# Two-level products from the first output block on, and a finished row scaled later

## The chip, the cores and the metric

The kernel runs on one core of a Trainium2 chip. The metric is the device time of one execution in microseconds; the median of three runs is 907.44 us (906.86 to 908.13). In the text PE is TensorE, DVE is VectorE, ACT is ScalarE, POOL is GpSimd and SP is SyncE, whose queue issues most of the transfers.

## The reference

With the sizes of this case (one sequence of 4096 frames, width 1024, one layer) only the pooling mixer is left. What is computed, in its essence:

```python
normed = rms_norm(x, norm_w)
u, gate = split(normed @ pool_in_w, 2)                # 1024 -> 2 x 1024
pooled = [trailing_mean(u_g, w) for w in (2, 4, 8, 16)] - u    # four groups of 256 channels
mixed = einsum('bsgc,gcd->bsgd', pooled, pool_group_w) + pool_group_b
h = x + (mixed * pool_scale * silu(gate)) @ pool_out_w         # 1024 -> 1024
out = rms_norm(h, final_norm_w)
```

All in float32.

## The kernel before

**Precision and products.** A float32 operand is split into a high and a low part, both in the type that TensorE multiplies at one column per step (`split`, line 203: the high part is a copy by ScalarE, the low part a subtraction by VectorE). A product is then three matmuls: high by high, high by low, low by high (`mm3`, line 802). Above that the kernel multiplies 2 x 2 blocks with seven products instead of eight (the Winograd form of Strassen's scheme). The seven are called P1 to P7; each needs sums of operand blocks, which VectorE forms, and the results are added up in PSUM and by VectorE and ScalarE.

**Stages.** The list `steps` (line 1439) has one entry for each product: stage a (input product, first half of the output columns) for four input blocks of 1024 frames, stage b (the second half) for the same four, then stage o (the output product) for eight output blocks of 512 frames. The order within an input block is P1, P2, P7, P6, P5, P4, P3 (`ORDER_IN`), within an output block P1, P7, P6, P2, P5, P4, P3 (`ORDER_OUT`). The main loop (line 1882) goes through the steps; at step n it issues the loads of a step some places ahead, the splits of the next one or two steps, and then the matmuls and evictions of step n. Pooling (`pool`, line 1060) runs between input and output: it takes the evicted input product and stores `yd`, which the output blocks load again. In the last input block (stage b, block 3) each step, once its product is done, also loads and splits the output weights of the same name into the same place (`load_w`, line 384).

**A second level.** Some products are themselves done with seven smaller products, so that 24 matmuls of 512 columns become 42 of 256. In the output stage P2 is done so from block 1 on (called the inner P2), and P7 from block 2 on (`OWN = 2`). The inner P2 takes three plain quarters and four sums of its operand (`split_inner`, line 890: four sums of 256 elements and the split of the plain operand; the split of the sums follows one step later, as `rest`). Its weights are three plain quarters of the split weight P2 and four sums, formed by `load_inner` (two loads from `wod`), `sum_inner` (four sums of 512 elements), `split_weight` (for each sum a copy by ScalarE and a subtraction by VectorE into a kept buffer, or, for P5, into a quarter of the weight's own place), and `end_weights` (the two raw buffers are given back). The products of the inner P2 go partly into the banks of the step (`sets["x"]`) and partly into two spare banks; `add_inner` (line 989) adds the spare banks to the rows. P5 and P6 of the inner level are done within the step P5 of the outer one, into a spare bank that `add_inner` has to read first.

**Buffers.** Eleven work buffers (`st`) and eight larger ones (`vt`) are handed out oldest first by `Slots`. `take` and `give` are calls of the program that issues the kernel, so a buffer that is taken again makes the new writer wait until the last reader of the old contents is done. `st.keep()` withdraws a buffer for good, as a home of inner weights; the list `gathered` holds them, three for P2 and, from block 1 on, three more for P7.

**Order.** Each engine works through a queue in order. The queue is written by a list scheduler (called the planner here) that follows a clock of its own: whenever an engine is free by that clock, it places the earliest instruction of the program whose inputs are there. `tc.issue_after` puts an instruction behind another of the same engine. From two steps ahead of output block 2 on, `InOrder.on` keeps the instructions of VectorE, ScalarE, POOL and SP in the order of the program; in the last block it is switched off in the step P2 (line 1607).

**The last block.** `steady` (line 1509) writes out the output blocks from 2 on and the last two steps of block 1. Rows of a finished block are scaled in the next one: `norm_row` (line 1261) multiplies a row group by its factor and the final weight on VectorE and has POOL store it. In the last block one of these, for the block before it, stands in the step P2 ahead of the product and its eviction. After the last product the rows of the last block are scaled by ScalarE and VectorE in halves and stored (`late_scalar`, `late_vector`).

Of the kernel before, what the change touches and what calls it, by code (L numbers as in the profile page):

```python
# [20 lines left out]
NB = S // TB  # L21
# [7 lines left out]
OWN = 2  # L29
# [57 lines left out]
def kernel(  # L87
# [57 lines left out]
    st = Slots(sts)  # L145
# [738 lines left out]
    def end_weights(i):  # L884
        for u in raws.pop(i)["held"]:
            give(u)
# [304 lines left out]

    def split_o(b, i):
        s = oxs[b]
        if i == P2 and b >= OWN - 1:
            return split_inner(s["12"])
        t = next_op("p (s a b) -> p s a b", s=2, a=4)
        if i == P7:
            s["3"] = take("p (a b) -> p a b", a=4)
            sub(s["3"], s["11"], s["21"])
        elif i == P6:  # L1200
            add(s["21"], s["21"], s["22"])
            sub(s["11"], s["21"], s["11"])
        elif i == P3:
            sub(s["12"], s["12"], s["11"])
            give(s.pop("11"))
        key = {P1: "11", P7: "3", P6: "11", P2: "12", P5: "21", P4: "22", P3: "12"}[i]
        split(t, s[key])
        if i not in (P1, P6, P2):
            give(s.pop(key))
        return t  # L1210
# [298 lines left out]
    def steady(n):  # L1509
# [58 lines left out]
        elif i == P6:  # L1568
            v = temp(0, "p (n k c) -> p n k c", n=4, k=2)
            sums_op = next_op("p (s n k c) -> p s n k c", s=2, n=4, k=2)  # L1570
            high(sums_op, v)
            low(sums_op, v)
            own_add()
            u = s.pop("21")
            give(u)
            if final:
                add_out(b, P6, sets, 0)
            norm_row(b - 1, 0, 0)
            if not final:
                norm_row(b - 1, 0, 1)  # L1580
            for m, p in enumerate((P7, P6, P5, P3)):
                ready[P2][p] = [sums_op[:, k, m] for k in range(2)]
            ready[P5] = next_op("p (s a b) -> p s a b", **whole)
            with tc.issue_after(latest[0]):
                out_part(P6, ready.pop(P6), sets["y"][1], 1, range(4))
            if final:
                partial["junk"] = temp(1, "p (a b) -> p a b", a=2)
                add_out(b, P6, sets, 1)
                split(ready[P5], u)
                for j in range(2):  # L1590
                    add_out(b, P7, sets, j)
            else:
                split(ready[P5], u)
                load_h(b, 1)
                evict_o(b, P7, sets)
                evict_o(b, P6, sets)
        elif i == P2:
            if not final:
                load_h(b, 0)
                ahead["11"] = load_y(c, 0, 0)  # L1600
                ahead["21"] = load_y(c, 1, 0)
            ready[P4] = next_op("p (s a b) -> p s a b", **whole)
            split(ready[P4], s["22"])
            give(s.pop("22"))
            if final:
                norm_row(b - 1, 0, 1)
            InOrder.on = not final
            product_out(P2, ready.pop(P2), sets, False)
            evict_o(b, P2, sets)
        elif i == P5:  # L1610
            sub(s["12"], s["12"], s["11"])
            give(s.pop("11"))
            ready[P3] = next_op("p (s a b) -> p s a b", **whole)
            split(ready[P3], s["12"])
            give(s.pop("12"))
            product_out(P5, ready.pop(P5), sets, False)
            evict_o(b, P5, sets)
        elif i == P4:
            if not final:
                ahead["12"] = load_y(c, 0, 1)  # L1620
                ahead["22"] = load_y(c, 1, 1)
                ready[P1] = next_op("p (s a b) -> p s a b", **whole)
                split(ready[P1], ahead["11"])
                u = temp(0, "p (a b) -> p a b", a=4)
                sub(u, ahead["11"], ahead["21"])
                ready["own"] = op_halves()
                high(ready["own"][1], u)
            product_out(P4, ready.pop(P4), sets, False)
            if final:
                evict_o(b, P4, sets)  # L1630
            else:
                add_out(b, P4, sets, 0)
        else:
            if not final:
                u = temp(0, "p (a b) -> p a b", a=4)
                v = temp(1, "p (n k c) -> p n k c", n=4, k=2)
                b11, b12, b21, b22 = row_quarters(u)
                square_rows(b, 1, sets, 0)
                sub(v[:, 0], b12, b11)
                sub(v[:, 1], b22, v[:, 0])  # L1640
                sub(v[:, 2], b22, b12)
                sub(v[:, 3], b21, v[:, 1])
                add_out(b, P4, sets, 1)
                sums_op = next_op("p (s n k c) -> p s n k c", s=2, n=4, k=2)
                high(sums_op, v)
                square_rows(b, 1, sets, 1)
                root(b, 1)
                plain_op, both = ready.pop("own")
                low(both, u)
                low(sums_op, v)  # L1650
                ready[P7] = {
                    p: [plain_op[:, k, g, j] for k in range(2)]
                    for p, (g, j) in {P1: (0, 0), P2: (1, 0), P3: (1, 1)}.items()
                }
                for m, p in enumerate((P5, P6, P7, P4)):
                    ready[P7][p] = [sums_op[:, k, m] for k in range(2)]
            product_out(P3, ready.pop(P3), sets, final)
            evict_o(b, P3, sets)
# [200 lines left out]
    def row_plan(b):  # L1859
# [8 lines left out]
        )  # L1868

    scales, summed = {}, []  # L1870
    forming = {
        (0, P4): lambda: load_inner(P2),
        (0, P3): lambda: sum_inner(P2),
        (1, P1): lambda: split_weight(P2, P7, P6),
        (1, P7): lambda: (split_weight(P2, P5, P4), end_weights(P2), load_inner(P7)),
        (1, P6): lambda: sum_inner(P7),
        (1, P5): lambda: split_weight(P7, P7, P6),
        (1, P4): lambda: (split_weight(P7, P5, P3), keep_temps(P7)),
    }
    forming_seven = (P7, P6, P5, P4)  # L1880

    for n in range(2, len(steps)):
# [15 lines left out]
            for j in rows.get(i, ()):  # L1898
                load_row(b + 1, j // 4, j % 4, early if b == 0 and i == P7 else None)
        if kind == "o":  # L1900
            while len(gathered) < (6 if b else 3 * (i in (P4, P3))) and st.free and len(st.free) + len(vt.free) > 4:
                gathered.append(st.keep())
                kept.append(gathered[-1])
            if b > 0 or i in (P4, P3):
                keep[0] = 0
        if kind == "o" and i == P6 and late_split:
            late_split.pop()()
        with ExitStack() as order:
            for ins in read_out.get(n - 2, {}).values():
                order.enter_context(tc.issue_after(ins))  # L1910
            advance("split", n, split_step, split_reach)
        if kind == "o" and (b, i) in forming:
            with tc.issue_after(latest_split[0]), tc.issue_after(latest_copy[0]):
                forming[b, i]()
        if n >= own_from - 2:
            InOrder.on = n == own_from - 2 or InOrder.on
            steady(n)
# [111 lines left out]
```

## Time and profile before

| what | value |
|---|---|
| median of three runs | 907.44 us |
| the profiled execution, its time | 907.23 us |
| the profiled execution, its span | 905.4 us |
| granted TensorE clock | 0.998 |
| PE busy | 895.8 us (99%) |
| DVE busy | 757.0 us (84%) |
| ACT busy | 517.5 us (57%) |
| POOL busy | 118.5 us (13%) |
| input stages a and b | from the start to 612.98 us |
| output stage | 612.98 us to the end |

A line of the timeline has the start in us from the start of the span, the duration, the engine, the line of the kernel and the operation, `out<-in` by the program's names without buffer numbers, the shape and the count; in brackets stands the idle time ahead of it and what ended that. Nearly all instructions of VectorE, ScalarE, POOL and SP carry line 79, that of the helper that records them, so they are told apart by engine, tiles and time. `bank` is a PSUM bank, `op` an operand's split buffer, `w` a split weight, `inner` a kept buffer with inner weights, `wod` the output weights in memory. PE's line 807 is a matmul of a whole product, line 949 one of the inner products. A row of the windows view has the window, its length, the busy time of PE, of PE's weight loads, of DVE, ACT and POOL, the granted clock, the share of the DMA engines and GB/s. In the chain of waits each piece is what the end of the program depended on at that time.

### The profile page before, as it was taken

The page shows a single profiled execution, that of the slowest core. Times are in us where ns is not written, and L with a number is a line of the kernel's source. Part 1 is how long each engine was busy: PE and PEld are TensorE (multiplying, and loading weights), DVE is VectorE, ACT ScalarE, POOL GpSimd, SP SyncE. Part 2 cuts the span into 40 slices and gives each one's busy share as a digit, 9 for nine tenths or more (in the row PEclk, how much of TensorE's full clock was granted, in tenths as well). Part 3 has the DMA queues.
Part 4 walks back from the last instruction along what each step waited for, and adds up shares of the span by engine and source line. Part 5 has one row for each costly group of instructions (what it writes and reads, how often), then busy time and mean ns, then how long its engine had stood idle before and what let it go on. Part 6 is the DMA issues. An engine that isn't in the chain of part 4 may idle for free.

```text
span 905.4 us, 12216 instructions
## 1 busy us (share of the span) xinstructions
PE 895.8 (99%) x4518; PEld 791.1 (87%) x4518; DVE 757.0 (84%) x925; ACT 517.5 (57%) x853; POOL 118.5 (13%) x208
## 2 busy tenths in 40 slices
PE   9999999999999999999999999999999999999996
PEld 7888888888888888889889888888889899999995
DVE  3899995985995999797599499599798878888797
ACT  7869547547445565346545636654657466565464
POOL 0020100100110000000000000001133333343330
PEclk9999999999999999999999999999999999999999
DMA  9987767577675453333554474638483865945953
GB/s 343 401 305 226 273 239 241 187 274 233 235 267 198 164 199 103 99 112 111 202 199 135 179 279 143 197 117 239 143 236 88 212 180 147 233 153 131 259 181 116
DMA packets 71692, 180.49 MB, mean 199 GB/s; under 512 B 6608, under 2 KB 24656, under 8 KB 71632
## 3 DMA queue, kind: packets, MB, share of 16 engines
q1 hardware_dynamic: 54976, 132.50, 42.6%
q0 software_dynamic: 15936, 46.16, 17.6%
q10 hardware_dynamic: 720, 1.06, 0.3%
q8 instruction: 35, 0.57, 0.3%
q14 instruction: 25, 0.20, 0.1%
HBM read 118.86 MB, written 60.83 MB: 198 GB/s over the span
## 4 chain that ended last, share of the span: by engine, by line
PE 87%; DVE 5%; ACT 3%; DMA 2%; issue 2%; POOL 0%; SPq 0%; DVEq 0%; ACTq 0%; POOLq 0%
PE bank L807 78%; PE bank L949 5%; DVE vt L79 2%; PE bank L753 2%; DVE op L79 2%; DMA st<-yd 1%; PE bank L447 1%; DVE st L79 1%; ACT op L79 1%; DMA early<-in_wut 1%; ACT st L79 1%; ACT w L79 0%; ACT vt L79 0%; DMA st<-wod 0%; DVE w L79 0%
## 5 line engine op out<-in xcount | busy, mean ns | idle before, releaser
L807 PE MATMUL bank<-op,w 128*128 128x512 f32 x2592 | 560.9, 379 | 0.1
L807 PEld LDWEIGHTS bank<-op,w 128*128 128x128 f32 x2592 | 489.4, 189 | 70.3 <-ACT vt L79 0.5
L807 PE MATMUL bank<-w,op 128*128 128x512 f32 (+1 forms) x1044 | 230.5, 377 | 0.0
L807 PEld LDWEIGHTS bank<-w,op 128*128 128x128 f32 x1044 | 192.3, 189 | 25.0
L79 DVE TENSOR_TENSOR op<-st,op 128x1024 fp32r<-128x1024 f32 x116 | 141.0, 1222 | 49.7 <-ACT op L79 49.3
L79 ACT ACTIVATE op<-st 128x1024 fp32r<-128x1024 f32 x116 | 121.4, 1051 | 68.7 <-PE bank L807 27.6
L79 ACT ACTIVATE op<-vt 128x1024 fp32r<-128x1024 f32 x67 | 70.4, 1053 | 59.3 <-DVE vt L79 38.7
L79 ACT ACTIVATE vt<-bank 128x512 f32<-128x512 f32 (+1 forms) x124 | 69.6, 580 | 48.0 <-PE bank L807 44.2
L79 DVE TENSOR_TENSOR op<-vt,op 128x1024 fp32r<-128x1024 f32 x67 | 80.9, 1221 | 17.5 <-ACT op L79 17.4
L79 DVE TENSOR_TENSOR st<-st,st 128x1024 f32<-128x1024 f32 (+1 forms) x55 | 63.9, 1181 | 17.6 <-ACT st L79 16.8
L79 POOL DMA_DIRECT2D vt<-in_x x26 | 23.3, 937 | 390.7 <-DVE vt L79 353.8
L79 ACT ACTIVATE bank<-bank 128x512 f32<-128x512 f32 (+1 forms) x78 | 38.7, 498 | 43.5 <-PE bank L807 32.1
L79 DVE TENSOR_TENSOR vt<-bank,vt 128x512 f32<-128x512 f32 (+1 forms) x94 | 54.2, 603 | 7.1 <-PE bank L949 4.6
L79 ACT ACTIVATE st<-bank 128x512 f32<-128x512 f32 (+1 forms) x58 | 33.0, 587 | 31.2 <-PE bank L807 17.4
L79 ACT ACTIVATE st<-st 128x1024 f32<-128x1024 f32 x33 | 34.8, 1056 | 22.6 <-DVE st L79 19.6
L79 DVE TENSOR_TENSOR st<-bank,st 128x512 f32<-128x512 f32 (+1 forms) x68 | 41.2, 625 | 7.4 <-PE bank L807 4.1
L79 DVE TENSOR_TENSOR st<-st,vt 128x1024 f32<-128x1024 f32 (+1 forms) x36 | 41.6, 1175 | 2.2 <-DMA vt<-rd 2.2
L949 PEld LDWEIGHTS bank<-w,op 128*128 128x128 f32 x312 | 40.4, 191 | 1.7
L949 PE MATMUL bank<-w,op 128*128 128x256 f32 x312 | 41.1, 275 | 0.0
L79 DVE TENSOR_TENSOR w<-st,w 128x1024 fp32r<-128x1024 f32 (+1 forms) x27 | 31.6, 1182 | 9.3 <-ACT w L79 9.2
L79 DVE TENSOR_TENSOR_SCAN vt<-vt,window 128x1040 f32<-128x1040 f32 x16 | 38.0, 2381 | 0.3 <-DMA yd<-vt 0.3
L79 DVE TENSOR_TENSOR vt<-vt 128x1024 f32<-128x1024 f32 (+3 forms) x42 | 37.6, 898 | 0.1
(115 smaller groups left out, 720.7 us busy)
## 6 DMA issues: line engine op xcount, KB each, us to landing
st<-in_xt SPq DMA_DIRECT2D x28, 512.0 KB, 6.2
sd<-st POOLq DMA_DIRECT2D x28, 512.0 KB, 4.4
st<-sd SPq DMA_DIRECT2D x26, 512.0 KB, 4.5
st<-in_x SPq DMA_DIRECT2D x21, 512.0 KB, 6.3
yd<-st SPq DMA_DIRECT2D x19, 512.0 KB, 2.9
vt<-yd SPq DMA_DIRECT2D x17, 512.0 KB, 10.4
out<-vt POOLq DMA_DIRECT2D x17, 512.0 KB, 3.3
st<-wod SPq DMA_DIRECT2D x16, 512.0 KB, 4.3
```

The costliest lines, as they stand in the source:

```text
L79: r = f(*args, **kwargs)
L447: latest[0] = nc.tensor.matmul(ps, a[:, kk, 2 * j + t, :], maps, start=t + m == 0, stop=t == 1 and m == len(pairs) - 1,).ins
L753: latest[0] = nc.tensor.matmul(cell(n, c).rearrange("p (a s) -> p a s", s=2), x1, x2, start=i == P1 and k + m == 0, stop=k == 1 and m == 2 ...
L807: latest[0] = nc.tensor.matmul(ps, a, b, start=start and n == 0, stop=stop and n == 2, skip_group_check=True).ins
L949: latest[0] = nc.tensor.matmul(ps, x1, x2, start=start and k + n == 0, stop=k == 1 and n == 2, skip_group_check=True,).ins
```

## The change

It has three parts.

- `split_o` returns `split_inner` for P2 in every output block, so block 0 too has an inner P2.
- What forms the weights of the inner P2 moves from the steps P4 and P3 of output block 0 and P1 and P7 of block 1 to the steps P1, P7, P5 and P4 of the last input block (stage b, block 3). The table `forming` has the stage in its keys for that. The three buffers for these weights are withdrawn in its step P5, by a new helper `gather`, where before they were withdrawn in the steps P4 and P3 of output block 0. The weights of the inner P7 are formed where they were.
- In the last block the `norm_row` of the block before it moves from the step P2 to the step P4, ahead of the product P4; it is issued after the order of the program has been switched off.

```diff
     def split_o(b, i):
         s = oxs[b]
-        if i == P2 and b >= OWN - 1:
+        if i == P2:
             return split_inner(s["12"])
...
             split(ready[P4], s["22"])
             give(s.pop("22"))
-            if final:
-                norm_row(b - 1, 0, 1)
             InOrder.on = not final
             product_out(P2, ready.pop(P2), sets, False)
             evict_o(b, P2, sets)
...
         elif i == P4:
-            if not final:
+            if final:
+                norm_row(b - 1, 0, 1)
+            else:
                 ahead["12"] = load_y(c, 0, 1)
...
+    def gather(count):
+        for _ in range(count):
+            gathered.append(st.keep())
+            kept.append(gathered[-1])
+
     forming = {
-        (0, P4): lambda: load_inner(P2),
-        (0, P3): lambda: sum_inner(P2),
-        (1, P1): lambda: split_weight(P2, P7, P6),
-        (1, P7): lambda: (split_weight(P2, P5, P4), end_weights(P2), load_inner(P7)),
-        (1, P6): lambda: sum_inner(P7),
-        (1, P5): lambda: split_weight(P7, P7, P6),
-        (1, P4): lambda: (split_weight(P7, P5, P3), keep_temps(P7)),
+        ("b", NB - 1, P1): lambda: load_inner(P2),
+        ("b", NB - 1, P7): lambda: sum_inner(P2),
+        ("b", NB - 1, P5): lambda: (gather(3), split_weight(P2, P7, P6)),
+        ("b", NB - 1, P4): lambda: (split_weight(P2, P5, P4), end_weights(P2)),
+        ("o", 1, P7): lambda: load_inner(P7),
+        ("o", 1, P6): lambda: sum_inner(P7),
+        ("o", 1, P5): lambda: split_weight(P7, P7, P6),
+        ("o", 1, P4): lambda: (split_weight(P7, P5, P3), keep_temps(P7)),
     }
...
         if kind == "o":
-            while len(gathered) < (6 if b else 3 * (i in (P4, P3))) and st.free and len(st.free) + len(vt.free) > 4:
-                gathered.append(st.keep())
-                kept.append(gathered[-1])
+            while b and len(gathered) < 6 and st.free and len(st.free) + len(vt.free) > 4:
+                gather(1)
...
-        if kind == "o" and (b, i) in forming:
+        if (kind, b, i) in forming:
             with tc.issue_after(latest_split[0]), tc.issue_after(latest_copy[0]):
-                forming[b, i]()
+                forming[kind, b, i]()
```

## The prediction

> **What bounds the kernel now.** I read the page first (busy shares, then the chain), and after it the timeline of PE, the windows view around each of PE's waits, and the timelines of DVE, ACT and SP there.
>
> ```profile
> PE 895.8 (99%) x4518; PEld 791.1 (87%) x4518; DVE 757.0 (84%) x925; ACT 517.5 (57%) x853; POOL 118.5 (13%) x208
> PE 87%; DVE 5%; ACT 3%; DMA 2%; issue 2%; POOL 0%; SPq 0%; DVEq 0%; ACTq 0%; POOLq 0%
> ```
>
> TensorE carries 87% of the chain and is nearly never idle, so a microsecond counts only if it shortens TensorE's work, removes one of its waits, or shortens the tail after its last matmul. In the output stage its timeline shows two waits:
>
> ```profile
> 612.98 51.96 PE L807 MATMUL bank<-w,op 128*128 128x512 f32 x240
> ...
> 668.12 2.75 PE L807 MATMUL bank<-w,op 128*128 128x512 f32 x12
> 671.19 0.94 PE L949 MATMUL bank<-inner,op 128*128 128x256 f32 x6 [0.31 <-DVE vt L79]
> ...
> 880.38 4.05 PE L807 MATMUL bank<-w,op 128*128 128x512 f32 x18
> 885.05 0.94 PE L949 MATMUL bank<-inner,op 128*128 128x256 f32 x6 [0.61 <-DVE vt L79]
> ...
> 887.78 10.61 PE L807 MATMUL bank<-w,op 128*128 128x512 f32 x60
> ```
>
> Block 0 runs whole (the first row: 240 matmuls, 0.216 us each). In block 1 and in the last block the inner product P6 waits for VectorE. It overwrites a bank that `add_inner` must first have read. The windows view, from the start of P2 to the start of P4, prices the three cases (columns: window, its length, then the busy time of PE, PEld, DVE, ACT, POOL):
>
> ```profile
> 628.52:638.88 10.36, 10.36 (x50) 9.07 (x48) 7.08 (x8) 3.68 (x5) 2.66 (x3) 1.00 1.09 285
> 664.78:675.23 10.45, 10.14 (x68) 9.15 (x67) 10.38 (x17) 5.72 (x10) 1.73 (x2) 1.00 1.07 270
> 735.92:745.78 9.86, 9.86 (x67) 9.22 (x66) 7.38 (x10) 3.78 (x6) 3.86 (x5) 1.00 0.93 249
> 877.04:887.78 10.74, 10.13 (x67) 9.14 (x66) 10.74 (x16) 2.12 (x2) 1.14 (x2) 1.00 0.45 162
> ```
>
> P2 and P5 take 10.36 us with a whole P2 (block 0), and 9.86 with an inner P2 that waits for nothing (block 3). Block 1 takes 10.45, so its inner P2 buys nothing; the last block takes 10.74. In those two VectorE is busy for 10.38 of 10.45 and 10.74 of 10.74 us.
>
> **The change, part by part.** The sum is made against the profiled execution (907.23 us, span 905.4). The median of the runs shown is 907.44, so I add 0.21 at the end.
>
> *Block 0's P2 becomes inner.* On TensorE 24 matmuls of 512 columns give way to 42 of 256: 10.36 - 9.86 = 0.50 us less if nothing waits. VectorE and ScalarE get work for it, priced by these groups (columns: busy time, mean of one in ns, idle before):
>
> ```profile
> L79 DVE TENSOR_TENSOR op<-vt,op 128x1024 fp32r<-128x1024 f32 x67 | 80.9, 1221 | 17.5 <-ACT op L79 17.4
> L79 ACT ACTIVATE op<-vt 128x1024 fp32r<-128x1024 f32 x67 | 70.4, 1053 | 59.3 <-DVE vt L79 38.7
> L79 DVE TENSOR_TENSOR vt<-bank,vt 128x256 f32<-128x256 f32 x29 | 11.5, 422 | 4.7 <-PE bank L949 4.6
> L79 DVE TENSOR_TENSOR inner<-st,inner 128x512 fp32r<-128x512 f32 x5 | 3.4, 686 | 0.0
> L79 ACT ACTIVATE inner<-st 128x512 fp32r<-128x512 f32 x5 | 3.1, 619 | 1.9 <-DMA out<-st 1.9
> ```
>
> `split_inner` adds four sums (4 x 0.42, by the 256-element row) and a second split (1.22 on VectorE, 1.05 on ScalarE); `add_inner` adds six sums (6 x 0.42): 5.4 us of VectorE. VectorE is full ahead of it:
>
> ```profile
> 592.26:612.98 20.72, 20.72 (x98) 18.14 (x96) 20.72 (x21) 12.16 (x16) 0.00 (x0) 1.00 0.34 117
> 612.98:628.52 15.54, 15.54 (x74) 13.61 (x72) 15.54 (x16) 7.33 (x10) 2.67 (x3) 1.00 0.77 222
> 628.52:649.24 20.72, 20.72 (x98) 18.14 (x96) 16.45 (x20) 9.88 (x19) 3.58 (x5) 1.00 0.67 177
> ```
>
> About 10 us of the second and third window is pooling of the last input block, which nobody needs before output blocks 6 and 7, so the extra work can displace it; but a queue is in order, and what stands ahead of the `add_inner` that frees the bank is PE's wait. Its bounds are 0 (block 3) and one pooling scan ahead of it, 38.0 us / 16 = 2.38:
>
> ```profile
> L79 DVE TENSOR_TENSOR_SCAN vt<-vt,window 128x1040 f32<-128x1040 f32 x16 | 38.0, 2381 | 0.3 <-DMA yd<-vt 0.3
> ```
>
> The nearest row is block 1, also with a full VectorE: 10.45 - 9.86 = 0.59. I take half of it, 0.30, since the weights' splits of block 1 are not in the way here. Net **-0.20**.
>
> *The weights' sums of P2 move* from output blocks 0 and 1 to input block 3: two loads of 512 KB on SP, four sums (0.69 each), four splits (0.69 on VectorE, 0.62 on ScalarE): 8 x 0.69 = 5.5 us of VectorE and 2.5 of ScalarE. There they meet free time:
>
> ```profile
> 571.54:592.26 20.72, 20.72 (x98) 18.14 (x96) 11.37 (x12) 11.12 (x16) 0.00 (x0) 1.00 0.69 222
> ```
>
> VectorE has 9.3 us idle and ScalarE 9.6, and the sums and the first two splits are issued there; only the last two (1.4 us) fall into the full window after it. Cost 0; if that cover is gone, 1.4 us of VectorE late, against operands that are some 6 us early in this stretch: the split for P5 of block 0 ends at 627.64, and P5 starts at 628.52 + 24 x 0.216 = 633.70.
>
> ```profile
> 626.43 1.21 DVE L79 TENSOR_TENSOR op<-st,op 128x1024 fp32r<-128x1024 f32 x1
> ```
>
> What leaves is 5.5 us: the sums (2.8) from the end of block 0, the splits (2.7) from block 1. Up to 649.24 VectorE has 4.3 us idle (20.72 - 16.45) for 1.4 + 5.4 - 2.8 = 4.0 us more, so block 0 hands no backlog on, and block 1 has 2.7 us less ahead of its wait of 0.59. The wait goes; from -0.59 to 0 I take **-0.50**.
>
> *Five work buffers are taken early*: two hold the raw sums from P1 to P4 of input block 3, three become homes of the weights from its P5 on (before: from P4 of output block 0). Followed through take and give, no step runs out, but loads get other buffers, freed later. On SP the moved loads pass the pooled stores and the other loads of output weights, all with steps to spare, except one place, where ScalarE stands just ahead of TensorE (chain of waits, then ACT's and VectorE's timelines):
>
> ```profile
> 555.99 3.40 DMA st<-wod
> ...
> 560.44 0.59 ACT vt L79
> ...
> 561.07 5.02 PE bank L807 x22
> ```
>
> ```profile
> 559.47 1.06 ACT L79 ACTIVATE w<-st 128x1024 fp32r<-128x1024 f32 x1 [5.88 <-DMA st<-wod]
> 560.44 1.07 ACT L79 ACTIVATE vt<-bank 128x512 f32<-128x512 f32 x2
> ```
>
> ```profile
> 554.75 1.22 DVE L79 TENSOR_TENSOR w<-st,w 128x1024 fp32r<-128x1024 f32 x1
> ...
> 557.02 2.35 DVE L79 TENSOR_TENSOR st<-st,st 128x1024 f32<-128x1024 f32 x2
> ```
>
> The first half of the output weight P2 is loaded at 555.99, when VectorE's split at 554.75 has freed its buffer; ScalarE waits 5.88 us for it, and behind that copy stand the evictions of input block 3's P2, without which P7 may not write the banks. Today that costs TensorE 0.2 us (P1 and P2 are 96 matmuls, 20.74 us, and take 20.94):
>
> ```profile
> 540.13:561.07 20.94, 20.88 (x97) 17.95 (x95) 20.81 (x21) 9.57 (x16) 0.00 (x0) 1.00 0.35 129
> ```
>
> With the sums' buffers taken, this load gets a buffer that the second of the two subtractions at 557.02 frees, at 559.37: 3.4 us later. If ScalarE's order stays, P7 starts 3.4 us late; if the planner now puts the evictions first, as it will where its own clock sees the load come later too, the 0.2 goes. Bounds -0.2 and +3.4; I take **0**.
>
> *The finished row of the last block* (`norm_row`, 1.28 us on VectorE, then a store by POOL) moves from ahead of P2's eviction to behind P5's:
>
> ```profile
> 882.18 1.28 DVE L79 SCALAR_TENSOR_TENSOR vt<-vt,ors,st 128x1024 f32<-128x1024 f32 x1
> 883.37 1.62 DVE L79 TENSOR_TENSOR vt<-bank,vt 128x512 f32<-128x512 f32 x3
> ...
> 895.20 0.41 DVE L79 SCALAR_TENSOR_TENSOR columns<-columns 128x1 f32<-128x1 f32 x2
> 895.76 0.69 DVE L79 TENSOR_TENSOR vt<-bank,vt 128x512 f32<-128x512 f32 x1
> ```
>
> The eviction whose last third frees P6's bank starts 1.2 us sooner, so TensorE's wait goes: 10.74 - 9.86 = 0.88 at most. But what is late next is VectorE itself. Its work up to the first addition of P3 at 895.76 is the same, only reordered, and it ends at 895.61: 0.15 us ahead. So I take **-0.16** for the tail, between -0.88 (the row drops behind the tail's chain) and +1.28 (it lands in that chain). POOL has no other work there, and the store falls where the DMA engines idle:
>
> ```profile
> 888.00:895.70 7.70, 7.70 (x38) 6.76 (x37) 7.34 (x26) 5.54 (x15) 0.00 (x0) 1.00 0.00 1
> ```
>
> Sum: -0.20 - 0.50 + 0 - 0.16 = -0.86: 906.37 for an execution like the profiled one, **906.6** for the median.
>
> A rule against the first step stands in the Trainium skill, "TensorE: Matmul & The Clock Gate", section "Back-to-back issue gap": in a real stream a matmul costs about 81 ns at 128 columns and 131 at 512, more per column the smaller it is. By it, an estimate on the line between them, 42 x 98 ns = 4.1 us against 24 x 131 = 3.1: the change would cost 1.0 us of TensorE. The trace does not agree: 0.216 us at 512 columns here.
>
> **The rivals.**
> 1. *Every wait goes, the tail too.* For it: all of TensorE's waits here are on VectorE or ScalarE work that the change moves. Against: VectorE's full 7.34 of 7.70 us before the tail. -0.50 - 0.59 - 0.2 - 0.88 = -2.17: 905.3. Faster.
> 2. *ScalarE stays blocked behind the later load, and P7 of input block 3 starts late* (the other side). For it: the wait of 5.88 us and the chain through it. It decides from the point where the copy of that weight still stands ahead of the first eviction. -0.86 + 3.4 = +2.54: 910.0. Slower.
> 3. *Block 1's wait only moves to block 0.* With 5.4 us more VectorE is full from 592 to about 649, and one scan ahead of `add_inner` costs 2.38 in place of 0.30: -0.86 + 2.08 = +1.2: 908.7, with block 1's own wait left as well 909.2. For it: the full windows; against it: the deferrable pooling.
> 4. *Half the columns, more than half the time.* If 42 matmuls cost the busy time of their rows, 0.83 us for a lone group of six (7 x 0.83 = 5.8) against 24 x 0.216 = 5.2, the inner product costs 0.6 and the first term turns from -0.20 to +0.9: 907.7. Against it: the clean 9.86 above. This is what the rule of the Trainium skill above amounts to here.
>
> **How the numbers follow.** Forecast 0.50 (906.6), rival 1 0.14, rival 2 0.18, rival 3 0.16 (a tenth of it slower by more than the bound), rival 4 0.02. A change of 0.2% (1.8 us) is about what a measurement of this kernel can tell from none. So faster 0.14, same 0.66, slower 0.20. The range takes in rival 1's time and rival 3's, and leaves out most of rival 2: 905.2 to 909.2. The forecast's own range is 905.7 to 907.6.
>
> **What would show it.** In the windows view block 0's P2 to P4 should last 9.9 to 10.5 us and block 1's 9.9. TensorE's wait in the last block should be gone, VectorE still full up to the first addition of P3, and the time from TensorE's last matmul to the end longer than today by what TensorE gained. P7 of input block 3 should start with no more than 0.2 us of wait. The prediction is wrong if TensorE waits there on ScalarE by over a microsecond, if a scan stands ahead of block 0's `add_inner`, or if the tail keeps its length and the whole 0.88 counts.

## The result, and the profile after

The changed kernel takes 914.47 us (median of six runs, 912.95 to 916.69) against 907.79 us (906.86 to 908.36) in the same comparison: 1.0080 times as long, 95% interval 1.0063 to 1.0096. The forecast was 906.6 us with a range to 909.2: wrong, and on the other side. The profiled execution is the fastest of the six, 912.95 us with a span of 911.2, so 5.8 us of span are to be found.

The page of the changed kernel, busy shares and chain by engine:

```profile
PE 897.5 (99%) x4536; PEld 792.3 (87%) x4536; DVE 762.1 (84%) x936; ACT 518.4 (57%) x854; POOL 118.7 (13%) x208
PE 82%; DVE 11%; DMA 2%; issue 2%; ACT 2%; SPq 0%; DVEq 0%; ACTq 0%
```

TensorE's share of the chain falls from 87% to 82%, VectorE's rises from 5% to 11%. The windows view tells where (columns as before: window, length, PE, PEld, DVE, ACT, POOL, granted clock). First two stretches of the kernel before that the prediction doesn't show, the last input block up to the output stage and the tail behind the last matmul:

```profile
540.13:612.98 72.85, 72.79 (x338) 63.42 (x336) 62.89 (x60) 40.82 (x57) 0.00 (x0) 1.00 0.46 156
898.40:905.40 7.00, 0.00 (x0) 0.00 (x0) 2.82 (x10) 2.31 (x7) 0.00 (x0) 0.75 0.54 202
```

and the changed kernel: last input block, P2 to P4 of block 0, of block 1 and of the last block, tail:

```profile
539.67:614.28 74.61, 73.57 (x337) 63.18 (x336) 66.42 (x66) 40.61 (x58) 0.00 (x0) 1.00 0.45 147
629.83:645.04 15.21, 11.58 (x68) 10.40 (x67) 11.88 (x15) 3.63 (x5) 0.88 (x1) 0.89 0.97 305
670.94:680.81 9.87, 9.87 (x68) 9.22 (x67) 8.52 (x15) 5.71 (x9) 0.86 (x1) 1.00 1.06 261
882.62:893.52 10.90, 10.13 (x67) 9.14 (x66) 10.90 (x17) 2.11 (x2) 0.60 (x1) 1.00 0.35 114
904.13:911.20 7.07, 0.01 (x1) 0.00 (x0) 2.82 (x10) 2.33 (x7) 0.00 (x0) 0.83 0.55 201
```

Against before: input block +1.76, block 0 +4.85 (15.21 - 10.36), block 1 -0.58 (9.87 - 10.45), last block +0.16, tail +0.07. With the 0.46 us by which this execution happened to be ahead at the first window, that is the 5.8.

**Block 0.** TensorE's timeline there, and the granted clock behind the wait:

```profile
633.17 2.76 PE L807 MATMUL bank<-w,op 128*128 128x512 f32 x12
639.55 1.65 PE L949 MATMUL bank<-inner,op 128*128 128x256 f32 x6 [3.63 <-DVE vt L79]
641.00 3.53 PE L807 MATMUL bank<-w,op 128*128 128x512 f32 x12
```

```profile
639.55:642.65 3.10, 3.10 (x11) 2.80 (x12) 1.72 (x4) 0.00 (x0) 0.00 (x0) 0.51 1.03 402
```

The leaf of P6 waits 3.63 us for VectorE. Then six matmuls that take 0.83 us elsewhere take 1.65, and the next twelve 3.53 instead of 2.76: the granted clock is 0.51 over the 3.10 us of the row. Wait (3.63) and slow stretch (1.6) are 5.2 of the 5.3 us over a block without a wait (9.87). VectorE's timeline shows what the leaf waited for:

```profile
632.90 1.41 DVE L79 SCALAR_TENSOR_TENSOR vt<-vt,colt,vt 128x512 f32<-128x512 f32 x2
634.23 1.21 DVE L79 SCALAR_TENSOR_TENSOR vt<-vt,vt 128x1024 f32<-128x1024 f32 x1
635.48 1.41 DVE L79 SCALAR_TENSOR_TENSOR st<-vt,colt,st 128x512 f32<-128x512 f32 x2
636.82 1.22 DVE L79 TENSOR_TENSOR op<-vt,op 128x1024 fp32r<-128x1024 f32 x1
637.95 1.22 DVE L79 TENSOR_TENSOR op<-st,op 128x1024 fp32r<-128x1024 f32 x1
639.08 0.41 DVE L79 TENSOR_TENSOR vt<-bank,vt 128x256 f32<-128x256 f32 x1
```

```profile
632.89 0.58 ACT L79 ACTIVATE vt<-bank 128x512 f32<-128x512 f32 x1
```

The last VectorE row is `add_inner(0, (0, 0))`. The row that it adds to was ready when ScalarE's copy ended, at 633.47. It stood 5.6 us in VectorE's queue: behind the end of the pooling (the first three rows) and the splits for P4 and P3. P4 starts at 645.04 and P3, 24 matmuls later, at about 650.2, so neither split was urgent. The rows stand back to back, none with a wait ahead of it: the order is the planner's, not that of the data (d7_part and d8_part_p3 below put it to the test).

**The last input block.** ScalarE's timeline, then TensorE's:

```profile
552.03 0.23 ACT L79 ACTIVATE vt<-tails 128x32 f32<-128x32 f32 x1 [5.95 <-DMA yd<-vt]
552.16 0.58 ACT L79 ACTIVATE bank<-bank 128x512 f32<-128x512 f32 x1
...
580.56 1.06 ACT L79 ACTIVATE w<-st 128x1024 fp32r<-128x1024 f32 x1 [2.82 <-DMA st<-wod]
...
582.47 1.55 ACT L79 ACTIVATE st<-bank 128x512 f32<-128x512 f32 x3
```

```profile
555.19 13.04 PE L807 MATMUL bank<-op,w 128*128 128x512 f32 x58 [0.84 <-ACT bank L79]
...
583.10 3.07 PE L807 MATMUL bank<-op,w 128*128 128x512 f32 x13 [0.19 <-ACT st L79]
```

A copy of 32 tail columns went to a buffer that a store was still reading; it waited 5.95 us, and the bank copies that TensorE needs stood behind it. In the kernel before the same copy ran without a wait (ScalarE's timeline before):

```profile
545.61 0.23 ACT L79 ACTIVATE vt<-tails 128x32 f32<-128x32 f32 x1
```

At 580 a weight split waited for its load with P6's evictions behind it. The buffers have changed places: the early weights hold two, and an output weight was loaded into one of the larger buffers (`vt`), which SP's timeline shows (in the kernel before, the loads of output weights in this stretch all went to `st`):

```profile
544.56 0.32 SPq L79 DMA_DIRECT2D vt<-wod  x1
```

**The last block.** TensorE's timeline:

```profile
885.97 2.97 PE L807 MATMUL bank<-w,op 128*128 128x512 f32 x13
889.71 0.94 PE L949 MATMUL bank<-inner,op 128*128 128x256 f32 x6 [0.77 <-DVE vt L79]
```

The row's scaling is gone from ahead of the addition, and the wait is still there, 0.77 us against 0.61. P6's leaf now stands behind 13 matmuls where it stood behind 18: this fits a planner that saw the addition come earlier and put the leaf earlier.

### The profile page after: what moved, and what is told of

It reads as the page before. It is cut to its first block, busy times and chain, and to the rows that moved or that the text cites. A ratio compares the mean times of both kernels' runs of the same rounds, so it can differ in the third digit from the quotient of the medians.

```text
span 911.2 us, 12265 instructions
## 1 busy us (share of the span) xinstructions
PE 897.5 (99%) x4536; PEld 792.3 (87%) x4536; DVE 762.1 (84%) x936; ACT 518.4 (57%) x854; POOL 118.7 (13%) x208
## 4 chain that ended last, share of the span: by engine, by line
PE 82%; DVE 11%; DMA 2%; issue 2%; ACT 2%; SPq 0%; DVEq 0%; ACTq 0%
PE bank L807 71%; PE bank L949 6%; DVE vt L79 4%; DVE op L79 3%; DVE st L79 3%; PE bank L447 3%; PE bank L753 2%; DMA st<-wod 1%; DVE w L79 1%; ACT st L79 1%; DMA early<-in_wut 1%; DMA vt<-wod 1%; ACT w L79 0%; ACT op L79 0%; DMA wod<-st 0%
## 5 line engine op out<-in xcount | busy, mean ns | idle before, releaser
L807 PE MATMUL bank<-w,op 128*128 128x512 f32 (+1 forms) x1020 | 226.5, 378 | 0.0
L79 DVE TENSOR_TENSOR st<-st,st 128x1024 f32<-128x1024 f32 (+2 forms) x59 | 65.6, 1132 | 17.7 <-ACT st L79 16.8
L79 POOL DMA_DIRECT2D st<-in_x x17 | 15.6, 974 | 377.4 <-ACT st L79 357.4
L79 DVE TENSOR_TENSOR vt<-bank,vt 128x512 f32<-128x512 f32 (+1 forms) x91 | 52.3, 601 | 10.7 <-PE bank L807 4.9
L79 DVE TENSOR_TENSOR st<-bank,st 128x512 f32<-128x512 f32 (+1 forms) x77 | 44.6, 602 | 5.4 <-PE bank L949 4.2
L949 PE MATMUL bank<-w,op 128*128 128x256 f32 x336 | 44.3, 275 | 0.0
L949 PE MATMUL bank<-inner,op 128*128 128x256 f32 x252 | 34.9, 279 | 4.4 <-DVE vt L79 4.4
```

The source lines that it names most:

```text
L79: r = f(*args, **kwargs)
L807: latest[0] = nc.tensor.matmul(ps, a, b, start=start and n == 0, stop=stop and n == 2, skip_group_check=True).ins
L949: latest[0] = nc.tensor.matmul(ps, x1, x2, start=start and k + n == 0, stop=k == 1 and n == 2, skip_group_check=True,).ins
```

## The experiments

All ratios are against the kernel before on the same chip.

### e1_row_moved: the row alone

```
# the kernel before, with the norm_row(b - 1, 0, 1) of the last block
# moved from the P1 step to the P4 step
```

> The kernel before with one part of the change alone: in the last block the finished row is scaled behind P5 instead of ahead of P2. The prediction's step priced this at -0.16 us (bounds -0.88 to +1.28), 907.1 us by the profiled run's 907.23. After the change's trace, where the wait ahead of P6's leaf is still there (0.77 us against 0.61 before) and the leaf stands behind 1 matmul of P5's second row where it stood behind 6, the theory is that the planner of the order used the freed 1.27 us of VectorE to put the leaf earlier, so the wait stays: between -0.1 and +0.3 us, the last block's window from P2 to P4 about 10.9 us (10.74 before). Rival: the moved row pushes the additions behind P5 and lengthens the tail behind the last matmul from 7.0 to 8.0 us or more, 908.3 us or more.

906.95 us against 907.08, ratio 1.0001 (0.9992 to 1.0010): no difference. The leaf again stands behind 13 matmuls and waits:

```profile
880.39 2.97 PE L807 MATMUL bank<-w,op 128*128 128x512 f32 x13
884.49 0.94 PE L949 MATMUL bank<-inner,op 128*128 128x256 f32 x6 [1.13 <-DVE vt L79]
```

The last block takes 11.27 us from P2 to P4 in this profile (10.74 before, 10.9 expected), the tail 7.08. The row's move costs and gains nothing that the runs can tell, within 0.1% either way.

### e2_weights_early: the weights' sums alone

```
 # the changed kernel
-        if i == P2:
+        if i == P2 and b >= OWN - 1:
 # and the last block's norm_row back at its old place
```

One of the weights' split parts lives in the place of the whole weight, so block 0's whole P2 multiplies partly overwritten weights here; the amount of work is the same.

> The change's middle part alone: the weights' sums of the output product P2 are formed in the last input block, block 0 keeps its whole P2 and the row of the last block stays where it was. Theory of separate places: the last input block is 1.8 us longer than before (74.6 us against 72.85 from its P1 to the output stage), block 0's P2 to P4 is 10.4 us as before, block 1's is 9.9 us (0.58 less): about 908.4 us. Rival one: block 0's wait comes from the early weights and their buffers and not from its inner P2: its window is 15 us here too, 913 us. Rival two: the last input block lengthens only together with an inner P2 in block 0 (whose operand is made there): 906.6 us.

908.36 us against 907.08, ratio 1.0015 (1.0007 to 1.0024). Input block, block 0, block 1:

```profile
539.93:613.73 73.80, 73.23 (x338) 63.27 (x337) 66.36 (x66) 40.51 (x57) 0.00 (x0) 1.00 0.44 150
629.27:639.63 10.36, 10.36 (x50) 9.07 (x49) 8.57 (x10) 3.68 (x5) 2.66 (x3) 1.00 1.06 267
665.53:675.40 9.87, 9.87 (x68) 9.23 (x67) 8.52 (x15) 5.71 (x9) 0.86 (x1) 1.00 1.04 254
```

The early sums cost the input block 0.95 us here and free block 1 of its wait; block 0 is as before. So block 0's loss needs its inner P2. The last block, whose row stands at its old place here, takes 11.44 us in this profile (877.21 to 888.65) against 10.74 in the kernel before's, so a difference of some tenths there, in one profile, needs a second profile.

### d3_pool_behind: all of the pooling behind block 0's additions

```
-        pool_due(n)
+        if (kind, b, i) != ("o", 0, P5):
+            pool_due(n)
         ...
         run(n)
+        # at ("o", 0, P5): pool_due(n), issued after P5's last addition
```

> The changed kernel with one difference: in output block 0 the pooling of the last input rows is issued behind the last addition of P5 instead of ahead of P5. Queue theory: the addition that P6's leaf waits for was ready at 633.5 us and stood until 639.1 us behind pooling and two splits in VectorE's queue; with the pooling behind it, it stands behind at most two splits, TensorE waits under 0.6 us there, no matmul of the block runs at half rate, and block 0's P2 to P4 takes 9.9 to 10.6 us instead of 15.2: 5 us off the change's time, 908 to 910 us. Rival one: the 256-column matmuls and the clock are what is slow in this block, the wait only follows: the window stays over 12 us, 911 us or more. Rival two: about 10 us of pooling stands now ahead of what P3 of block 0 and P1 of block 1 need, and TensorE waits there instead: 911 to 914 us.

916.12 us, ratio 1.0096 (1.0082 to 1.0110). Block 0 has lost its wait, and TensorE waits in block 1 (TensorE's timeline):

```profile
630.51:640.38 9.87, 9.87 (x68) 9.22 (x67) 5.10 (x8) 3.62 (x5) 0.86 (x1) 1.00 0.99 233
```

```profile
657.86 5.48 PE L807 MATMUL bank<-w,op 128*128 128x512 f32 x24 [1.35 <-DVE op L79]
665.38 6.70 PE L807 MATMUL bank<-w,op 128*128 128x512 f32 x22 [2.03 <-DVE op L79]
```

Rival two, then, and by more than its 914: the inner P2 itself is as fast as promised and the order was the cause of block 0's wait, but about 10 us of pooling in one piece are then waited for at block 1's operands. VectorE was busy for 5.10 of the 9.87 us, time that it lacked afterwards.

### g1_tail: and the tail copies behind P7's evictions

```
-                copy(v[:, :, 0:HIST], tails[:, g])
+                with tc.issue_after(filled[0]):   # P7's last eviction, last input block
+                    copy(v[:, :, 0:HIST], tails[:, g])
```

> As the kernel before this one of the list (pooling behind the last addition of P5), and one more difference: in the last input block ScalarE's copies of the tail columns for the pooled rows are issued behind P7's evictions instead of as early as they fit. Theory: the copy into a buffer that was still being stored (5.95 us of wait at 552.0 us) held P2's two bank copies back and cost TensorE about 1.1 us at 552 to 555 us; that goes, the two smaller gaps of 0.25 and 0.45 us at 565.4 and 582.5 us, where late weight loads stand ahead of evictions, stay: 1.0 to 1.3 us less than the run with the pooling alone, 906.8 to 908.8 us. Rival: the bank copies were late for another reason (the weight loads of P1 behind them), and the gap stays: no change against the pooling alone.

914.48 us, ratio 1.0080 (1.0066 to 1.0094), 1.6 us less than the one before; but the profile doesn't bear the theory out. The gap at 555 us is gone, and the one at P6 has grown, so that the input block takes 74.64 us against 73.88:

```profile
583.35 6.96 PE L807 MATMUL bank<-op,w 128*128 128x512 f32 x31 [1.28 <-ACT st L79]
```

What the one queue entry gave, the late weight load behind it took. The intervals of the two overlap, and the two profiled executions took about the same (916.29 and 916.12), so whether the 1.6 us are a difference is open.

### e1b_row_leaf: the row, with P6's leaf held where it was

```
 # e1_row_moved, in the last block
+                    out_part(i, t, ps[1], 1, range(2))   # six matmuls of row 1 first
                 product_inner(P6)
```

> The kernel before with the moved row (as e1_row_moved) and one thing more: in the last block the leaf of P6 is held behind six matmuls of P5's second row, where it stood in the kernel before. In e1_row_moved the planner had put it behind one, and TensorE waited 1.30 us there (0.77 in the kernel before). Theory: the row's move does make the addition about 1.2 us earlier, and only the earlier leaf gave it back; with the leaf held, the wait is under 0.3 us and the last matmul comes 0.5 to 1.0 us earlier than in the kernel before: 906.1 to 906.6 us against 907.1. Rival: VectorE stays the limit with the leaf where it was and the wait stays above 0.6 us, or the tail grows by what the wait loses: 907.0 us, no difference.

907.63 us against 907.02, ratio 1.0003 (0.9993 to 1.0014). P6's leaf waits next to nothing, P5's leaf takes the wait over (TensorE's timeline, then VectorE's):

```profile
887.90 0.94 PE L949 MATMUL bank<-w,op 128*128 128x256 f32 x6 [1.02 <-DVE vt L79]
```

```profile
886.24 1.27 DVE L79 SCALAR_TENSOR_TENSOR vt<-vt,ors,st 128x1024 f32<-128x1024 f32 x1
887.43 1.20 DVE L79 TENSOR_TENSOR vt<-bank,vt 128x256 f32<-128x256 f32 x3
```

The planner had put the row (886.24) right ahead of the next additions. The rival's outcome, by another mechanism than either named.

### d7_part: three pooling operations behind block 0's additions

```
+            if later is not None and g == 1:      # pooling due at ("o", 0, P5)
+                later.append(rest_of_group)       # issued after P5's last addition
```

> The changed kernel with one difference: of the pooling in output block 0 only the last three operations of the second group (1.22, 0.75 and 0.75 us, 2.9 us in all at 634.2 to 636.8) are issued behind P5's last addition; all pooling ahead of them stays where it is. Queue theory: the addition stands 2.9 us earlier, the wait of 3.8 us shrinks to about 1.0 us, the matmuls behind it run at full rate, and as only 2.9 us of VectorE work move into block 1's time, nothing there waits more than 0.5 us: about 4 us off the change's time, 910 to 911 us. Rival: VectorE has no idle time left in blocks 0 and 1, and what leaves block 0 is waited for in block 1, as with all of the pooling moved (stalls of 1.5, 2.2, 0.3 and 1.4 us there): 913 us or more.

908.77 us against 907.02, ratio 1.0025 (1.0016 to 1.0033). 2.6 us less of pooling ahead of the addition (634.23 to 636.82 in the changed kernel's rows) shorten the wait by 2.5 us, and no slow matmuls follow:

```profile
636.24 0.94 PE L949 MATMUL bank<-inner,op 128*128 128x256 f32 x6 [1.10 <-DVE vt L79]
```

Nothing waits in block 1. The queue theory holds. The gain, 5.0 us by the ratios (1.0080 to 1.0025), is more than expected: the slow stretch of 1.6 us went with the wait, and the input block took 73.5 us in this profile (613.50 - 540.00), 1.1 less than in the changed kernel's, with the same order there.

### d8_part_p3: and P3's operand behind the addition

```
+            if (kind, b, i) == ("o", 0, P5):
+                order.enter_context(tc.issue_after(seen["vector"]))
```

> As d7_part, and the operand of block 0's P3 (its sum and its split) is issued behind the addition that P6's leaf waits for. Queue theory: the addition stands another 1.1 to 2.3 us earlier, nothing waits for P3's operand until 645 us, so the wait goes altogether and block 0's P2 to P4 takes 9.9 to 10.2 us: 1.0 to 1.5 us less than d7_part, 909 to 910 us, of which 1 to 1.8 us over the kernel before are the last input block's. Rival: the later P3 operand or the three late pooling operations make P3 or block 1 wait: as d7_part or slower.

907.83 us against 907.02, ratio 1.0007 (0.9998 to 1.0016). Windows of the input block and of block 0, then VectorE's row of the addition:

```profile
539.86:614.18 74.32, 73.31 (x337) 63.18 (x336) 66.44 (x66) 40.51 (x57) 0.00 (x0) 1.00 0.44 148
629.72:639.59 9.87, 9.87 (x68) 9.22 (x66) 8.75 (x13) 3.78 (x5) 0.88 (x1) 1.00 0.94 245
```

```profile
634.13 0.41 DVE L79 TENSOR_TENSOR vt<-bank,vt 128x256 f32<-128x256 f32 x1
```

The addition runs at 634.13 in place of 639.08 and block 0 is free of waits. The same work in another order is worth 5.3 us by the profiles (15.21 to 9.87) and 6.6 by the ratios (1.0080 to 1.0007), most of the change's loss. Of what is left over the kernel before in this profile the largest piece is the input block, +1.47.

### d9_split_early: and the weights' splits two steps earlier

```
-        ("b", NB - 1, P5): lambda: (gather(3), split_weight(P2, P7, P6)),
-        ("b", NB - 1, P4): lambda: (split_weight(P2, P5, P4), end_weights(P2)),
+        ("b", NB - 1, P6): all of these
```

> As d8_part_p3, and the weights' splits of the last input block are issued two steps earlier (at P6, all four together, where they stood at P5 and P4), so that the two buffers of the loaded weights come free earlier. Theory: the last input block's 1.0 to 1.8 us come from ScalarE standing at weight loads whose buffers came free late, with TensorE's evictions behind it (0.45 us at 582.5 in the change, 1.44 in g1_tail); the earlier splits put P6's evictions ahead of the late load, and VectorE has 5.5 us less to do in its full stretch from 593 us on: the gap at 582 to 584 goes, the one at 553 to 556 stays: 0.4 to 0.8 us less than d8_part_p3, 908.2 to 909.5 us. Rival: the three buffers that the split weights take are missed two steps earlier and the gaps grow: slower than d8_part_p3.

909.73 us against 907.02, ratio 1.0028 (1.0018 to 1.0038): slower than d8_part_p3. In the profile the input block takes 74.91 us, 0.6 more, and block 0 is 0.9 longer up to P4. The gap at 582 us is gone, the same load stands in front of the next pair of evictions:

```profile
587.12 5.23 PE L807 MATMUL bank<-op,w 128*128 128x512 f32 x23 [1.08 <-ACT st L79]
```

ScalarE's queue was the right place to look and the remedy wrong: buffers freed earlier don't help where the order still puts a loaded weight ahead of an eviction.

### k1_b3: the input block's evictions first

```
 # d8_part_p3, with g1_tail's order, and for the output weights of P2 and P6:
+            with tc.issue_after(evicted[0]):   # behind the same step's evictions
                 split(w[i][h], u)
```

> As d8_part_p3, with two differences in the last input block: ScalarE's copies of the tail columns for the pooled rows are issued behind P7's evictions (as in g1_tail), and the splits of the output weights of P2 and P6 are issued behind the evictions of the same step. Theory: the block's 1.0 to 1.8 us over the kernel before are ScalarE's queue: a tail copy into a buffer still being stored, and weight splits whose loads came late, each with evictions behind it. With the evictions ahead, the gaps at 555, 566 and 583 us (1.0, 0.1 and 0.35 us, with the slower first matmuls 1.75 us in all in d8_part_p3) go, and block 3's P1 to the output stage takes 72.8 to 73.1 us: 906.0 to 906.6 us, 0.5 to 1.0 us less than the kernel before. Rival: the late loads come to hold something further on (the splits' place is taken at the start of the output stage), as each part that was moved so far: 907.3 us or more.

906.10 us against 907.27, ratio 0.9989 (0.9980 to 0.9997). Input block, block 0, block 1:

```profile
539.62:612.14 72.52, 72.52 (x337) 63.50 (x336) 65.43 (x65) 40.85 (x57) 0.00 (x0) 1.00 0.44 150
627.68:637.55 9.87, 9.87 (x67) 9.13 (x66) 8.75 (x11) 3.79 (x5) 0.88 (x1) 1.00 0.97 231
663.46:673.33 9.87, 9.87 (x67) 9.22 (x66) 9.61 (x16) 5.72 (x9) 2.02 (x3) 1.00 1.05 238
```

In none of the three does TensorE wait. The late loads hold nothing further on. With the order of two queues put right, the change's first two parts gain: 0.49 in block 0 and 0.58 in block 1, which they were meant to, and 0.33 in the input block, 1.4 us by these rows against before.

### m1_last: the last block alone, row behind the last addition

```
 # e1b_row_leaf
+                with tc.issue_after(seen["vector"]):
                     norm_row(b - 1, 0, 1)
```

> The last block alone: the kernel before with the leaf of P6 held behind six matmuls (as e1b_row_leaf), and the moved row issued behind the last of P5's additions, where e1b_row_leaf had it between two of them (TensorE waited 1.19 us at P5's leaf there). Theory: the row is then out of the way of both leaves, the waits of the last block fall from 0.87 us to under 0.4 us together, and the 1.2 us of the row fall into VectorE's time behind 890 us, where it waits for TensorE now and then: 906.2 to 906.7 us. Rival: that time isn't idle, the last rows' scaling comes later by as much, the tail behind the last matmul grows from 7.0 to 7.5 us or more: 907.0 us or more.

906.83 us against 907.27, ratio 0.9996 (0.9987 to 1.0005). Last block and tail:

```profile
876.71:887.11 10.40, 10.26 (x67) 8.98 (x66) 10.37 (x17) 2.11 (x2) 0.73 (x2) 1.00 0.28 112
897.72:905.40 7.68, 0.01 (x1) 0.00 (x0) 3.58 (x14) 2.99 (x8) 0.00 (x0) 0.81 0.58 216
```

TensorE gains 0.34 us (10.74 to 10.40), the tail grows by 0.68 (7.00 to 7.68). The rival has it: VectorE is full, and TensorE's gain comes back behind its last matmul.

### n_all: k1_b3 and m1_last together

> k1_b3 and m1_last together: the change with block 0's addition ahead of pooling and of P3's operand, the last input block's evictions ahead of the late copies and splits, and the last block's leaf and row as in m1_last. If both theories hold the effects add up: block 0 -0.5, block 1 -0.6, last block -0.5 us against the kernel before: 905.3 to 906.0 us. If only the one or the other holds, 906.2 to 906.8 us; if neither, 907 us or more.

905.35 us against 907.27, ratio 0.9979 (0.9970 to 0.9988): the one version that is faster than the kernel before by about 0.2%. Its interval overlaps with that of k1_b3, so whether the last block's part adds anything is open. In its profile the last block takes 10.10 us (876.15 to 886.25), 0.64 less than before, and the tail 7.64, 0.64 more: the exchange of m1_last again.

### after_again: the changed kernel, a second profile

> The changed kernel once more, for a second profile: its runs lie between 912.95 and 916.69 us, and the first profile is of the fastest. Theory: block 0's wait is there in the same place with the same instructions ahead of the addition, and the runs differ by the length of the stretch of half-rate matmuls behind that wait and by the waits of the last input block, which hang on DMAs: block 0's P2 to P4 14.5 to 18 us, the last input block 73.8 to 75.5 us. Rival: the slower runs lose elsewhere, and block 0 stays within 0.3 us of 15.2 us.

914.47 us (two runs), ratio 1.0079 (1.0061 to 1.0098). Block 0 from P2 to P4:

```profile
630.57:646.05 15.48, 11.81 (x68) 10.43 (x66) 11.93 (x15) 3.64 (x5) 0.88 (x1) 0.89 0.97 300
```

The same wait (3.67 us) and the same slow stretch; 15.48 lies within both the theory's range and the rival's, so it doesn't decide between them. The input block took 74.44 us. Of the 1.1 us of span over the first profile, 0.27 are block 0's; 0.9 arose before the last input block. Why the changed kernel's runs scatter over 3.7 us is not settled. Their mean granted clocks point at the slow stretch: 0.997 in the two profiled executions, but 0.994 in five of the other six (914.24 to 916.69 us), while no run of d8_part_p3 is below 0.998. An estimate from that: 0.003 of 912 us is 2.7 us more lost to the clock. None of those five was profiled.

## Why the prediction was wrong, step by step

*Block 0's P2 becomes inner (forecast -0.20, measured +4.85).* This step failed, in the price of the wait that the change adds. The 0.50 us of TensorE are there (9.87 against 10.36 in d8_part_p3 and k1_b3), and the place was named, but the wait was put at 0.30 with one scan, 2.38, as its upper bound. It was 3.63, and the slower clock after it, for which the sum had no term, added 1.6. Three things went wrong. The nearest row, block 1, was taken for its full VectorE, without reading which instructions would stand ahead of the addition in block 0. The bound counted one instruction, where six, none of them a scan, stood there with nothing to hold them back. And the 4.3 us idle for 4.0 us more were a budget over 20 us, while the addition had to run within the 2.3 us between 633.47 and 635.76, when the 12 matmuls ahead of the leaf were through (633.17 + 12 x 0.216).

VectorE's rows before would have priced it. In block 0 its queue ran dry when a split ended at 633.82, 5.3 us after the start of P2 (628.52); the next row waits for ScalarE:

```profile
632.60 1.22 DVE L79 TENSOR_TENSOR op<-st,op 128x1024 fp32r<-128x1024 f32 x1
635.47 1.23 DVE L79 TENSOR_TENSOR op<-st,op 128x1024 fp32r<-128x1024 f32 x1 [1.66 <-ACT op L79]
```

The step itself puts 2.9 us of operand sums and split ahead of the addition, and the late weight splits 1.4. If the addition goes to the end of that queue, an estimate of its turn is 9.6 us after the start of P2 (it was 9.25: 639.08 - 629.83), where 5.5 was needed: a wait of some 4 us. Rival 3 was this mechanism, with the chance too low and the price too small; its dearer form also took block 1's wait to go on, which it didn't.

*Rival 4, and the rule of the Trainium skill on small matmuls.* An inner P2 without a wait takes 9.87 us in block 0 of d3_pool_behind, d8_part_p3 and k1_b3; the row of block 3 was the right one. This stands against the rule of the Trainium skill, "TensorE: Matmul & The Clock Gate", "Back-to-back issue gap", as the prediction said.

*Block 1's wait (forecast -0.50, measured -0.58).* Right: e2_weights_early shows that the early weights alone bring it.

*Five work buffers taken early (forecast 0, bounds -0.2 to +3.4, measured +1.76, and +0.65 to +1.59 in the other profiles that keep this part).* The mechanism, ScalarE standing at a late buffer with evictions behind it, was right; the place was not. The load that the prediction followed cost little (P7 took 10.62 us against 10.47), as the planner put all but the last eviction of that step ahead of it. Two others cost: the tail copy (P1 and P2 took 22.10 us against 20.94) and the weight of P6 (P6 and P5 took 21.18 against 20.72). They were not followed, although the step said that "loads get other buffers, freed later". k1_b3, where evictions go first, takes the step's cost to -0.33, a little below the lower bound.

*The weights' sums in idle time (forecast 0).* Right as a matter of capacity: VectorE takes 3.5 us more in the input block (66.42 against 62.89) and no gap there is VectorE's.

*The finished row (forecast -0.16, bounds -0.88 to +1.28, measured +0.16 and +0.07 in the tail).* The reason given was right, that VectorE's total work is the limit; m1_last shows the exchange directly, 0.34 gained and 0.68 given back, and n_all once more. That the wait would go was wrong: the planner moved the leaf up by five matmuls (e1_row_moved). The measured +0.16 itself is too small to read from one profile of each.

The chance of 0.20 for slower was the forecast's other fault: two independent steps each hung on an order that the planner writes anew, and each could cost several microseconds and gain half a one.

## What to carry to other kernels

Price a wait that a change adds by listing what will stand in that engine's queue between the time its operands are ready and the time it is needed; a free-time budget over a longer window, or one instruction as a bound, says nothing where an order is planned by other costs. When a planner writes the order, an edit of one line also moves instructions that it doesn't touch (a leaf, a copy of 32 columns, a buffer's next owner), so compare the two orders before trusting a term. And look in the changed trace for work that runs early with nobody waiting for it: here three pooling operations and one split, put behind the addition with the sum that the split reads, were worth 5.3 us in the profiles.

## What the hardware showed that was not expected

A wait can cost more than itself. After 3.63 us of wait in the changed kernel, and after 3.67 in its second profile, TensorE's granted clock was about half of full for some 3 us (0.51 in the row above), which cost 1.6 us more for the same matmuls. An estimate of the length, if the clock is half in the slow stretch and full beside it: (1 - 0.57) x 4.00 / 0.5 = 3.4 us by this row of the second profile.

```profile
640.30:644.30 4.00, 3.96 (x13) 3.39 (x14) 1.76 (x4) 0.00 (x0) 0.00 (x0) 0.57 1.04 407
```

After waits of 1.10 us (d7_part) and 1.35 us (d3_pool_behind) it stayed at 1.00. At about 2 us both happened. Behind the wait of 2.03 us in d3_pool_behind the clock fell, behind one of the same length in g1_tail, and a later one of 2.25 us there, it didn't:

```profile
666.50:669.60 3.10, 3.10 (x9) 2.41 (x8) 2.25 (x3) 1.21 (x2) 2.43 (x5) 0.51 0.97 256
```

```profile
665.00:670.00 5.00, 5.00 (x24) 4.41 (x25) 4.11 (x7) 2.17 (x4) 4.41 (x7) 1.00 1.02 278
```

The Trainium skill, "TensorE: Matmul & The Clock Gate", "Part 1: The HAM clock gate", says that the array falls to half rate after an idle window of about 3.4 us, and that this window runs freely. The two waits of over 3.6 us agree with it. The wait of 2.03 us, after which the clock fell once and not the other time, is shorter than the stated window; what decided there is open.
